# Weight sums of a seven-product matrix pair: from VectorE additions to accumulating DMA transfers

## The chip, the cores and the metric

The kernel runs on one core of a Trainium2 chip. The metric is the device time of one execution in microseconds, from the program's first to its last instruction on the core, with what the launch adds around it. Engines are named as in the profile: PE is TensorE's matrix multiply, DVE is VectorE, ACT is ScalarE, POOL is GpSimd, and SP is the engine whose queue issues most DMA transfers.

## The reference

One inference step of a two-layer decoder trunk for 536 tokens (16 learned tokens, 512 of a prompt, 8 of a sample group). Each layer has a half feed-forward block, a recurrent mixer and a second half feed-forward block, so there are four feed-forward blocks of this form:

```python
def half_ffn(x, g, w_gate, w_up, w_down):
    h = rmsnorm(x, g)
    return 0.5 * ((jax.nn.silu(h @ w_gate) * (h @ w_up)) @ w_down)
```

The model width is 1024 and the hidden width 2816, all in float32. The change touches only how `h @ w_gate` and `h @ w_up` are formed.

## The kernel before

Every float32 product is made of three matrix multiplies with rounded operands. A weight tile is split into a rounded high part (`whi`, a cast on ACT) and a remainder (`wlo`, a subtraction on DVE), and likewise the activations (`hh`, `hl`). `block_mm` then issues high times high, high times low and low times high (lines 328 to 330).

A feed-forward block walks over 22 column tiles of 128 hidden units, in pieces of 8, 8 and 6; after each piece come four items that multiply with `w_down`. The first four column tiles of a block are done plainly (`run_plain`), the other 18 with a scheme of seven half products in place of eight (`seven_item` and `run_seven`). So each block has groups of 4, 8 and 6 such tiles in a row, and the program has 72. Such a tile is called an item below. Its gate weights g and up weights u are loaded as two tiles of 512 KB (`raw`, or `rawx` for every second item), each with two halves g0, g1 and u0, u1 of 128 by 512 numbers. The scheme needs the weights w (g0 and g1), u1, and the sums

- t1 = g0 + u0,
- t2 = t1 + u1,
- t4 = t2 + g1,
- s = u0 + u1.

All four sums are made on DVE, by `sums_a` (lines 342 and 343) and `sums_b` (lines 348 and 349), into one tile `wsum`; `split` turns each into a high and a low part.

The seven products of an item stand on PE in a fixed order, called P1 to P7 here, each of 12 matrix multiplies. They run over PSUM banks a, b and c. Bank a takes P1, P3, P5 and P7, and between them it is read out: by `keep` (line 484, a copy on ACT) after P1 and after P3, by line 507 on DVE after P5, and by line 513 on ACT after P7. P2 goes to bank b, which line 496 reads on DVE. P4 and P6 go to bank c. While one item is multiplied, the steps of the next one (its sums and splits) are called one after another between the products by `nstep`, and `load_next` issues the load of the item after that into the raw tiles that have come free.

The kernel gives the program order; the tile framework's scheduler then lays down a fixed order for each engine, which can differ from the order of the calls. An engine takes its instructions strictly in that order: one that waits holds up everything queued behind it.

Of the kernel before, what the change touches and what calls it, by code (L numbers as in the profile page):

```python
# [11 lines left out]
F32 = mybir.dt.float32  # L12
# [3 lines left out]
ALU = mybir.AluOpType  # L16
# [89 lines left out]
def trunk(ctx, tc, A, O):  # L106
    nc = tc.nc
    P = 128
    cnt = [0]

    def til(pool, shape, tag, dt=F32, bufs=None):
        cnt[0] += 1
        kw = {} if bufs is None else {"bufs": bufs}
        return pool.tile(shape, dt, tag=tag, name=f"{tag}_{cnt[0]}", **kw)
# [17 lines left out]
    def bank(tag="m"):  # L132
        return til(rings[tag][0], [P, 512], tag)
# [135 lines left out]
    ext = {}  # L269
    turn = {"raw": 0, "whi": 0, "wlo": 0}  # L270

    def wtile(tag):
        n = turn[tag]
        turn[tag] = n + 1
        dt = F32 if tag == "raw" else F32R
        if ext and n % 4 > 1:
            return til(ext["pool"], [P, 2, 512], f"{tag}x", dt, bufs=2)
        return til(wpool, [P, NK, P], tag, dt, bufs=2).rearrange("p (h k) m -> p h (k m)", h=2)
# [4 lines left out]
    def split_w(src):  # L283
        n = src.shape[1]
        hi, lo = wtile("whi")[:, :n], wtile("wlo")[:, :n]
        nc.scalar.copy(hi, src)
        nc.vector.tensor_sub(lo, src, hi.bitcast(F32))  # L287
        return hi, lo

    def load_pair(it, srcs, nk):  # L290
        it.raw = [wtile("raw") for _ in srcs]
        for t, src in zip(it.raw, srcs):
            dst = t.rearrange("p h (k m) -> p (h k) m", m=P)[:, :nk]
            nc.sync.dma_start(dst, src.rearrange("(k p) m -> p k m", p=P))
# [25 lines left out]
    def pair_item(wg, wu, j):  # L320
        return plain_item([w[:, 128 * j:128 * j + 128] for w in (wg, wu)], NK)


    def block_mm(o, u, nk, rh, rl, start, stop):
        hi, lo = u
        kw = {} if start else {"skip_group_check": True}
        for k in range(nk):
            nc.tensor.matmul(o, hi[:, k], rh(k), start=start and k == 0, stop=False, **kw)  # L328
            nc.tensor.matmul(o, hi[:, k], rl(k), start=False, stop=False, **kw)  # L329
            nc.tensor.matmul(o, lo[:, k], rh(k), start=False, stop=stop and k == nk - 1, **kw)  # L330
# [3 lines left out]
    def seven_item(wg, wu, j):  # L334
        it = Item()
        it.w = {}
        it.load = lambda: load_pair(it, [w[:, 128 * j:128 * j + 128] for w in (wg, wu)], NK)

        def sums_a():
            g, u = it.raw  # L340
            it.t = t = til(ext["pool"], [P, 4, 512], "wsum", bufs=1)
            nc.vector.tensor_add(t[:, 1], g[:, 0], u[:, 0])
            nc.vector.tensor_add(t[:, 0], t[:, 1], u[:, 1])

        def sums_b():
            g, u = it.raw
            t = it.t
            nc.vector.tensor_add(t[:, 2], u[:, 0], u[:, 1])
            nc.vector.tensor_add(t[:, 3], t[:, 0], g[:, 1])

        def split(name, src):
            def fn():
                it.w[name] = split_w(src())
            return fn

        it.steps = [sums_a, split("w", lambda: it.raw[0]), split("t", lambda: it.t[:, 0:2]), sums_b]
        it.late = [split("s", lambda: it.t[:, 2:4]), split("u", lambda: it.raw[1][:, 1:2])]
        return it

    def ffn(l, pre, rstd, first=None, done=None, start=None, tokens=PARTS, scaled_end=None):  # L360
# [5 lines left out]
        n = a1 - a0  # L366
        t1, t2, tl = slice(a0, a1), slice(b0, b1), slice(a0, b1)
# [6 lines left out]
        def flush():  # L374
            while pending:
                pending.pop(0)()
# [3 lines left out]
        with tc.tile_pool(name="ffn", bufs=2) as fp:  # L380
# [5 lines left out]
            def hidden(gt, ut):  # L386
                h = gtile(F32R)
                hid.append(h)

                def fn():  # L390
                    nc.vector.tensor_mul(ut[:, tl], ut[:, tl], gt[:, tl])
                    nc.scalar.copy(h[:, 0, tl], ut[:, tl])
                    nc.vector.tensor_sub(h[:, 1, tl], ut[:, tl], h[:, 0, tl].bitcast(F32))

                pending.append(fn)
# [69 lines left out]
            def run_seven(it, j, nxt):  # L465
                gt, ut = til(fp, [P, T], "gt"), til(fp, [P, T], "ut")
                bank_of = {}

                def product(b, name, i, rh, rl, first, last):
                    if first:  # L470
                        bank_of[b] = bank("d")[:, :n]
                    u = tuple(z[:, i].rearrange("p (k m) -> p k m", m=P) for z in it.w[name])
                    block_mm(bank_of[b], u, 4, rh, rl, first, last)
                    return bank_of[b]

                def half_x(h, ts):
                    return (lambda k: hh[:, 4 * h + k, ts]), (lambda k: hl[:, 4 * h + k, ts])

                def half_s(i):
                    return (lambda k: Z["h"][:, i, k]), (lambda k: Z["l"][:, i, k])  # L480

                def keep(ps):
                    s = til(fp, [P, n], "part", bufs=4)
                    nc.scalar.copy(s, ps)  # L484
                    return s

                def nstep():
                    if nxt is not None and nxt.steps:
                        nxt.steps.pop(0)()

                pa = product("a", "w", 0, *half_x(0, t1), True, True)
                s1 = keep(pa)
                it.late[0]()
                flush()
                pb = product("b", "w", 1, *half_x(1, t1), True, True)
                nc.vector.tensor_add(gt[:, t1], pb, s1)
                nc.scalar.activation(gt[:, t1], gt[:, t1], AF.Silu)
                it.late[1]()
                pa = product("a", "t", 0, *half_s(1), False, True)
                s2 = keep(pa)  # L500
                load_next()
                nstep()
                pc = product("c", "t", 1, *half_s(0), True, True)
                s3 = keep(pc)
                nstep()
                pa = product("a", "s", 0, *half_s(2), False, True)
                nc.vector.tensor_add(ut[:, t2], pa, s3)
                nstep()
                pc = product("c", "u", 0, *half_s(3), False, True)
                nc.vector.tensor_add(ut[:, t1], pc, s2)  # L510
                nstep()
                pa = product("a", "s", 1, *half_x(1, t2), False, True)
                nc.scalar.activation(gt[:, t2], pa, AF.Silu)
                hidden(gt, ut)

# [21 lines left out]
            for k0, k1 in PIECES:  # L537
                for j in range(k0, k1):
                    if j < PLAIN:
                        it = first if j == 0 and first is not None else pair_item(wg, wu, j)  # L540
                        items.append((it, lambda it, nxt, j=j: run_plain(it, j, nxt)))
                    else:
                        items.append((seven_item(wg, wu, j), lambda it, nxt, j=j: run_seven(it, j, nxt)))
                if k1 == FT:
                    def close(it, nxt):
                        sp.close()
                        if scaled_end is not None:
                            scaled_end()

                    items.append((None, close))  # L550
                for parts in ([tokens[:1], tokens[1:]] if ends and k1 == FT else [tokens]):
                    for m in range(0, NK, 2):
                        srcs = [wd[128 * k0:128 * k1, 128 * (m + i):128 * (m + i) + 128] for i in range(2)]
                        items.append((plain_item(srcs, k1 - k0),
                                      lambda it, nxt, k0=k0, k1=k1, m=m, parts=parts: run_down(it, k0, k1, m, parts, nxt)))
# [5 lines left out]
            def load_next():  # L561
                if loads:
                    loads.pop(0).load()
# [1107 lines left out]
```

## Time and profile before

| | |
|---|---|
| median of 3 runs | 2327.33 us (2322.22 to 2327.39) |
| the profiled execution | 2327.36 us |
| its span, first to last instruction | 2325.6 us |
| PE busy | 2275.5 us, 98% of the span |
| DVE busy | 1669.8 us, 72% |
| ACT busy | 1080.4 us, 46% |
| POOL busy | 142.0 us, 6% |

The profiled execution stands at the median of the runs; 1.8 us of it lie around the span. Busy shares are averages over stages with different limits: the feed-forward blocks, the mixers and the ends have to be read apart.

### The profile page before, as it was taken

To read this page: it belongs to the slowest core of one execution; us is meant where nothing else is said; L and a number is where in the kernel's file an instruction comes from. 1 tells how busy PE (TensorE), PEld (TensorE's weight loads), DVE (VectorE), ACT (ScalarE), POOL (GpSimd) and SP (SyncE) were. 2 spreads that over 40 slices of the span, in tenths; PEclk is the share of its full clock that TensorE was granted. 3 is DMA by queue.
4 is the path that set the end of the run, shared out by engine and by line. 5 is a ranking of instruction groups with operands and counts; after the bars stand their busy time and mean duration, and the time that the engine had idled before them with its cause. 6 is when DMAs were issued, how large, how long until landed. Compare 5 with 4: busy or idle time off the path is not lost. (4 is left out here: it accounts for less than half of the span.)

```text
span 2325.6 us, 45180 instructions
## 1 busy us (share of the span) xinstructions
PE 2275.5 (98%) x18368; PEld 2226.7 (96%) x18368; DVE 1669.8 (72%) x2980; ACT 1080.4 (46%) x2040; POOL 142.0 (6%) x192
## 2 busy tenths in 40 slices
PE   8999999999999999999999999999999999999998
PEld 8999999989998988999999999999999989999998
DVE  7858476696656787966757885847666877958576
ACT  6525254373343456434535452525433455525355
POOL 0000000312212100000000000000021200000000
PEclk9999999999999999999999999999999999999999
DMA  6323334222222116242423332333344454233324
GB/s 177 109 74 103 90 96 135 82 66 79 79 71 70 49 41 174 70 121 75 118 75 99 91 110 81 101 92 95 116 120 116 124 166 141 85 98 100 109 85 135
DMA packets 417849, 233.71 MB, mean 100 GB/s; under 512 B 19397, under 2 KB 408838, under 8 KB 417641
## 3 DMA queue, kind: packets, MB, share of 16 engines
q1 hardware_dynamic: 416920, 229.40, 34.1%
q8 instruction: 144, 2.36, 0.4%
q10 hardware_dynamic: 720, 1.42, 0.2%
q14 instruction: 65, 0.52, 0.1%
HBM read 215.81 MB, written 14.97 MB: 99 GB/s over the span
## 5 line engine op out<-in xcount | busy, mean ns | idle before, releaser
L234 PE MATMUL d<-hh,whi 128*128 128x264 f32 (+2 forms) x1136 | 343.7, 303 | 5.8 <-ACT whi L222 3.8
L236 PE MATMUL d<-hh,wlo 128*128 128x264 f32 (+2 forms) x1136 | 327.0, 288 | 1.8 <-DVE wlo L223 1.7
L235 PE MATMUL d<-hl,whi 128*128 128x264 f32 (+2 forms) x1136 | 326.3, 287 | 1.4 <-DVE hl L1404 1.4
L329 PE MATMUL d<-hl,whi 128*128 128x268 f32 (+1 forms) x832 | 238.4, 287 | 1.8 <-DVE hl L187 1.7
L328 PE MATMUL d<-hh,whi 128*128 128x268 f32 (+1 forms) x832 | 237.3, 286 | 1.7 <-ACT hh L186 1.2
L330 PE MATMUL d<-hh,wlo 128*128 128x268 f32 (+1 forms) x832 | 237.6, 286 | 0.5 <-DVE wlo L287 0.5
L234 PEld LDWEIGHTS d<-hh,whi 128*128 128x128 f32 x1136 | 216.2, 190 | 11.5 <-ACT whi L222 5.1
L236 PEld LDWEIGHTS d<-hh,wlo 128*128 128x128 f32 x1136 | 215.3, 190 | 4.8 <-DVE wlo L223 4.1
L235 PEld LDWEIGHTS d<-hl,whi 128*128 128x128 f32 x1136 | 216.2, 190 | 1.8 <-DVE hl L1404 1.6
L528 DVE SCALAR_TENSOR_TENSOR xT<-d,xT 128x272 f32<-128x272 f32 (+2 forms) x192 | 83.0, 434 | 167.0 <-PE d L330 166.9
L328 PE MATMUL d<-hid,whi 128*128 128x264 f32 (+2 forms) x704 | 201.5, 287 | 0.0
L328 PE MATMUL d<-hid,whix 128*128 128x264 f32 (+2 forms) x704 | 201.1, 286 | 0.0
L329 PE MATMUL d<-hid,whix 128*128 128x264 f32 (+2 forms) x704 | 200.8, 285 | 0.0
L329 PE MATMUL d<-hid,whi 128*128 128x264 f32 (+2 forms) x704 | 200.7, 286 | 0.0
L330 PE MATMUL d<-hid,wlox 128*128 128x264 f32 (+2 forms) x704 | 200.6, 285 | 0.0
L330 PE MATMUL d<-hid,wlo 128*128 128x264 f32 (+2 forms) x704 | 200.4, 285 | 0.0
L222 ACT CAST whi<-raw 128x512 fp32r<-128x512 f32 (+1 forms) x158 | 99.0, 662 | 160.6 <-PE d L235 103.2
L328 PE MATMUL d<-sumh,whix 128*128 128x268 f32 (+1 forms) x576 | 170.3, 296 | 0.2 <-ACT part L484 0.2
L328 PE MATMUL d<-sumh,whi 128*128 128x268 f32 (+1 forms) x576 | 164.4, 285 | 0.0
L330 PE MATMUL d<-sumh,wlo 128*128 128x268 f32 (+1 forms) x576 | 164.2, 285 | 0.0
L329 PE MATMUL d<-suml,whi 128*128 128x268 f32 (+1 forms) x576 | 164.2, 285 | 0.0
L329 PE MATMUL d<-suml,whix 128*128 128x268 f32 (+1 forms) x576 | 163.9, 285 | 0.0
(381 smaller groups left out, 6699.0 us busy)
## 6 DMA issues: line engine op xcount, KB each, us to landing
raw<-in_ffn_gate_dram SPq DMA_DIRECT2D x44, 512.0 KB
raw<-in_ffn_up_dram SPq DMA_DIRECT2D x44, 512.0 KB
rawx<-in_ffn_gate_dram SPq DMA_DIRECT2D x44, 512.0 KB
rawx<-in_ffn_up_dram SPq DMA_DIRECT2D x44, 512.0 KB
raw<-in_ffn_down_dram SPq DMA_DIRECT2D x32, 512.0 KB
rawx<-in_ffn_down_dram SPq DMA_DIRECT2D x32, 512.0 KB
raw<-in_even_w_in_dram SPq DMA_DIRECT2D x30, 512.0 KB
raw<-in_odd_w_in_dram SPq DMA_DIRECT2D x25, 512.0 KB
```

Source lines behind the costliest of these rows:

```text
L222: nc.scalar.copy(hi[:, ks], raw[:, ks])
L234: nc.tensor.matmul(o, hi[:, k], h, start=(k == 0), stop=False)
L235: nc.tensor.matmul(o, hi[:, k], l, start=False, stop=False)
L236: nc.tensor.matmul(o, lo[:, k], h, start=False, stop=(k == nk - 1))
L328: nc.tensor.matmul(o, hi[:, k], rh(k), start=start and k == 0, stop=False, **kw)
L329: nc.tensor.matmul(o, hi[:, k], rl(k), start=False, stop=False, **kw)
L330: nc.tensor.matmul(o, lo[:, k], rh(k), start=False, stop=stop and k == nk - 1, **kw)
L528: nc.vector.scalar_tensor_tensor(xv[:, sl], ps, -0.5, xv[:, sl], ALU.mult, ALU.add)
```

## The change

One sum, t1, is still made on DVE (line 343 of the changed kernel). The other three are made in place by DMA transfers that POOL issues and that add what they carry to what lies at their destination:

- s: half u1 is added onto half u0 within the raw tile of u (line 344),
- t2: once t1 has been split, half u1 is added onto the tile that holds t1 (line 359),
- t4: once t2 has been split, half g1 is added onto the same tile (line 359 again).

The sum tile shrinks from four halves to one, and there are two of them in turn. The splits become: t1, w, t2 during the item before, and u (both halves, now s and u1) and t4 during the item's own products. The third and fourth product now use t2 and t1 under their own names, in the same order as before.

```diff
-        def sums_a():
-            g, u = it.raw
-            it.t = t = til(ext["pool"], [P, 4, 512], "wsum", bufs=1)
-            nc.vector.tensor_add(t[:, 1], g[:, 0], u[:, 0])
-            nc.vector.tensor_add(t[:, 0], t[:, 1], u[:, 1])
-
-        def sums_b():
-            g, u = it.raw
-            t = it.t
-            nc.vector.tensor_add(t[:, 2], u[:, 0], u[:, 1])
-            nc.vector.tensor_add(t[:, 3], t[:, 0], g[:, 1])
-
-        def split(name, src):
+
+        def first_sum():
+            g, u = it.raw
+            it.t = til(ext["pool"], [P, 512], "wsum")
+            nc.vector.tensor_add(it.t, g[:, 0], u[:, 0])
+            nc.gpsimd.dma_start(u[:, 0], u[:, 1], accum_op=ALU.add)
+
+        def split(name, i):
             def fn():
-                it.w[name] = split_w(src())
+                if i is not None:
+                    it.w[name] = split_w(it.raw[i])
+                    return
+                n = 0 if name != "t2" else 1
+                if n == 0:
+                    it.slot = wtile("whi"), wtile("wlo")
+                hi, lo = (z[:, n] for z in it.slot)
+                it.w[name] = tuple(z[:, n:n + 1] for z in it.slot)
+                nc.scalar.copy(hi, it.t)
+                nc.vector.tensor_sub(lo, it.t, hi.bitcast(F32))
+                if name != "t4":
+                    nc.gpsimd.dma_start(it.t, (it.raw[1] if name == "t1" else it.raw[0])[:, 1], accum_op=ALU.add)
             return fn
 
-        it.steps = [sums_a, split("w", lambda: it.raw[0]), split("t", lambda: it.t[:, 0:2]), sums_b]
-        it.late = [split("s", lambda: it.t[:, 2:4]), split("u", lambda: it.raw[1][:, 1:2])]
+        it.steps = [first_sum, split("t1", None), split("w", 0), split("t2", None)]
+        it.late = [split("u", 1), split("t4", None)]
...
-                it.late[1]()
-                pa = product("a", "t", 0, *half_s(1), False, True)
+                nstep()
+                pa = product("a", "t2", 0, *half_s(1), False, True)
                 s2 = keep(pa)
                 load_next()
-                nstep()
-                pc = product("c", "t", 1, *half_s(0), True, True)
+                it.late[1]()
+                pc = product("c", "t1", 0, *half_s(0), True, True)
...
-                pa = product("a", "s", 0, *half_s(2), False, True)
+                pa = product("a", "u", 0, *half_s(2), False, True)
...
-                pc = product("c", "u", 0, *half_s(3), False, True)
+                pc = product("c", "u", 1, *half_s(3), False, True)
...
-                pa = product("a", "s", 1, *half_x(1, t2), False, True)
+                pa = product("a", "t4", 0, *half_x(1, t2), False, True)
```

**DVE in the middle of a group of eight.** The first block, second group: the item being multiplied has the tiles `gt_338` and `ut_339` and the banks `d_340`, `d_344` and `d_351`. Before the change, over the length of one item, from the first sum of the next item (`wsum_350`) on:

```order
L342 TENSOR_TENSOR wsum_350_2534<-raw_328_2401,raw_329_2402 128x512
L348 TENSOR_TENSOR wsum_350_2534<-raw_329_2402 128x512
L393 TENSOR_TENSOR hid_337_2472<-ut_319_2345,hid_337_2472 128x536
L496 TENSOR_TENSOR gt_338_2473<-d_344_2497,part_341_2488 128x268
L343 TENSOR_TENSOR wsum_350_2534<-wsum_350_2534,raw_329_2402 128x512
L287 TENSOR_TENSOR wlo_354_2553<-raw_328_2401,whi_353_2552 128x1024
L349 TENSOR_TENSOR wsum_350_2534<-wsum_350_2534,raw_328_2401 128x512
L287 TENSOR_TENSOR wlo_356_2570<-wsum_350_2534,whi_355_2569 128x1024
L507 TENSOR_TENSOR ut_339_2474<-d_340_2475,part_352_2570 128x268
L510 TENSOR_TENSOR ut_339_2474<-d_351_2537,part_347_2528 128x268
```

After the change, at the same item. `wsum_325` is its own sum tile, `wsum_345` that of the next item and `wsum_365` that of the item after next; line 357 subtracts in a split of t1, t2 or t4, line 287 in one of w or u:

```order
L357 TENSOR_TENSOR wlox_350_2554<-wsum_325_2401,whix_349_2553 128x512
L502 TENSOR_TENSOR gt_338_2493<-d_344_2517,part_341_2508 128x268
L357 TENSOR_TENSOR wlo_354_2573<-wsum_345_2532,whi_353_2572 128x512
L343 TENSOR_TENSOR wsum_365_2663<-rawx_347_2549,rawx_348_2550 128x512
L287 TENSOR_TENSOR wlo_356_2591<-raw_327_2418,whi_355_2590 128x1024
L513 TENSOR_TENSOR ut_339_2494<-d_340_2495,part_352_2570 128x268
L357 TENSOR_TENSOR wlo_354_2573<-wsum_345_2532,whi_353_2572 128x512
L516 TENSOR_TENSOR ut_339_2494<-d_351_2557,part_346_2547 128x268
L287 TENSOR_TENSOR wlox_363_2642<-raw_328_2419,whix_362_2641 128x1024
L397 TENSOR_TENSOR ut_339_2494<-ut_339_2494,gt_338_2493 128x536
L399 TENSOR_TENSOR hid_357_2623<-ut_339_2494,hid_357_2623 128x536
L357 TENSOR_TENSOR wlox_370_2685<-wsum_345_2532,whix_369_2684 128x512
```

Three additions per item have gone. The first sum has moved ahead: before, it was that of the next item and stood ahead of the read-out of bank b; now it is that of the item after next and stands between the next item's t1 split and its w split, ahead of the read-out of bank a (line 513, line 507 before). The splits of t1, t2 and t4 of one tile stand 4 and 5 rows apart.

**ACT at the same place after the change,** from the item's own t4 cast (`whix_349`) to the read-out of bank a after P7 (line 519). Line 356 casts t1, t2 or t4, line 286 w or u, and line 490 is the copy in `keep`:

```order
L356 CAST whix_349_2553<-wsum_325_2401 128x512
L356 CAST whi_353_2572<-wsum_345_2532 128x512
L503 ACTIVATE gt_338_2493<-gt_338_2493 128x268
L490 COPY part_346_2547<-d_340_2495 128x268
L286 CAST whi_355_2590<-raw_327_2418 128x1024
L490 COPY part_352_2570<-d_351_2557 128x268
L356 CAST whi_353_2572<-wsum_345_2532 128x512
L286 CAST whix_362_2641<-raw_328_2419 128x1024
L519 ACTIVATE gt_338_2493<-d_340_2495 128x268
```

The next item's t1 cast now stands right behind this item's t4 cast, and its t2 cast ahead of its u cast; before, there was one cast for two sums in each of two places.

**POOL over the same stretch after the change** (before, it had nothing in the feed-forward blocks): every row is one accumulating transfer of 256 KB.

```order
L359 DMA wsum_325_2401<-rawx_308_2288 128x512
L344 DMA raw_328_2419<-raw_328_2419 128x512
L359 DMA wsum_325_2401<-rawx_307_2287 128x512
L359 DMA wsum_345_2532<-raw_328_2419 128x512
L344 DMA rawx_348_2550<-rawx_348_2550 128x512
L359 DMA wsum_345_2532<-raw_327_2418 128x512
```

Three transfers per item have come, in the order t2 of the next item, s of the item after next, t4 of the next item.

## Rows read from the trace of the kernel before

**Rows 1.** The page, part 1: busy us (share of the span) xinstructions.

```profile
PE 2275.5 (98%) x18368; PEld 2226.7 (96%) x18368; DVE 1669.8 (72%) x2980; ACT 1080.4 (46%) x2040; POOL 142.0 (6%) x192
```

**Rows 2.** Busy time by stretch: length, busy (instructions) of each engine, PEclk, DMA.

```profile
200.00:400.00 200.00, 200.00 (x1610) 198.67 (x1610) 135.68 (x203) 90.00 (x140) 1.78 (x4) 1.00 0.35 105
400.00:600.00 200.00, 193.46 (x1547) 182.96 (x1546) 147.97 (x294) 98.94 (x207) 48.56 (x72) 1.00 0.27 77
...
1200.00:1400.00 200.00, 200.00 (x1605) 198.90 (x1605) 156.93 (x237) 103.29 (x161) 0.00 (x0) 1.00 0.35 100
```

**Rows 3.** Instructions on the sum tile: duration ns min/median/max, first and last start.

```profile
L342 DVE TENSOR_TENSOR wsum<-raw,raw x36: 682/687/700, 57.2 to 2249.3; 128x512 f32<-128x512 f32 x36
...
L342 DVE TENSOR_TENSOR wsum<-rawx,rawx x36: 683/686/693, 73.8 to 2259.5; 128x512 f32<-128x512 f32 x36
```

**Rows 4.** Timeline of PE: P1, P3, P7 of one item, the next P1.

```profile
1117.41 0.29 PE L328 MATMUL d<-hh,whi 128*128 128x268 f32 x1
...
1120.37 0.29 PE L328 MATMUL d<-sumh,whi 128*128 128x268 f32 x1
...
1126.43 0.29 PE L328 MATMUL d<-hh,whix 128*128 128x268 f32 x1
...
1127.91 0.28 PE L328 MATMUL d<-hh,whi 128*128 128x268 f32 x1
```

**Rows 5.** Timeline of ACT in the same item: start us, us, what, [idle before].

```profile
1117.49 0.62 ACT L286 CAST whix<-rawx 128x512 fp32r<-128x512 f32 x1 [0.37 <-PE d L329]
...
1120.49 1.05 ACT L286 CAST whi<-raw 128x1024 fp32r<-128x1024 f32 x1 [0.21 <-PE d L329]
...
1126.56 1.05 ACT L286 CAST whix<-wsum 128x1024 fp32r<-128x1024 f32 x1 [1.77 <-issue]
```

**Rows 6.** Timeline of DVE in the same item.

```profile
1118.29 0.69 DVE L287 TENSOR_TENSOR wlox<-rawx,whix 128x512 fp32r<-128x512 f32 x1
...
1119.52 0.69 DVE L342 TENSOR_TENSOR wsum<-raw,raw 128x512 f32<-128x512 f32 x1
...
1121.35 0.43 DVE L496 TENSOR_TENSOR gt<-d,part 128x268 f32<-128x268 f32 x1
1121.70 0.68 DVE L343 TENSOR_TENSOR wsum<-wsum,raw 128x512 f32<-128x512 f32 x1
1122.30 1.22 DVE L287 TENSOR_TENSOR wlo<-raw,whi 128x1024 fp32r<-128x1024 f32 x1
1123.43 0.69 DVE L349 TENSOR_TENSOR wsum<-wsum,raw 128x512 f32<-128x512 f32 x1
...
1127.64 1.23 DVE L287 TENSOR_TENSOR wlox<-wsum,whix 128x1024 fp32r<-128x1024 f32 x1 [0.57 <-ACT whix L286]
```

**Rows 7.** Timeline of SP's queue: four transfers at their issue.

```profile
355.40 0.34 SPq L1465 DMA_DIRECT2D xd<-xT  x1
...
592.52 0.40 SPq L1073 DMA_DIRECT2D acc<-in_state_rwkv_dram  x1
...
654.28 0.39 SPq L1073 DMA_DIRECT2D acc<-in_state_rwkv_dram  x1
...
1031.83 0.37 SPq L294 DMA_DIRECT2D raw<-in_ffn_up_dram  x1
```

**Rows 8.** Timelines of POOL and DVE: the instructions that waited for the last three.

```profile
595.60 1.28 POOL L1077 TENSOR_TENSOR sq<-acc,sq 128x512 f32<-128x512 f32 x1 [33.88 <-DMA acc<-in_state_rwkv_dram]
...
657.48 1.27 POOL L1077 TENSOR_TENSOR sq<-acc,sq 128x512 f32<-128x512 f32 x1 [19.30 <-DMA acc<-in_state_rwkv_dram]
...
1035.91 0.69 DVE L342 TENSOR_TENSOR wsum<-raw,raw 128x512 f32<-128x512 f32 x1 [2.87 <-DMA raw<-in_ffn_up_dram]
```

**Rows 9.** DMA by quarter us after the first: length, PEclk, DMA share, GB/s.

```profile
356.25:356.50 0.25, 1.00 0.93 360
356.50:356.75 0.25, 1.00 1.01 394
356.75:357.00 0.25, 1.00 0.83 326
```

## The prediction

> **What bounds the kernel now.** I read the page's busy times first: PE is busy for 2275.5 of 2325.6 us, DVE for 1669.8 [rows 1]. Then I read busy times by stretch, because an average hides which stage has gaps. In the feed-forward stretches PE is busy for 200.00 of 200 us, with DVE at 136 to 157; only mixer stretches leave PE idle, 6.5 us in the one shown [rows 2]. All 72 changed items lie where PE has no gap. One item takes 10.50 us from its P1 to the next one's P1 on PE [rows 4]. DVE work taken away there shortens nothing; the question is whether the new transfers make PE wait.
>
> **What the change removes.** Three of four additions on DVE, 0.69 us each [rows 3], issued 0.60 us apart (1121.70 to 1122.30 in [rows 6]): 1.8 us per item, 130 us over 72. PE covers all of it, so I put it at nothing. It would be worth something only where PE waits for DVE. ACT's and DVE's columns for the splits are the same as before, and PE's work is unchanged.
>
> **What it adds: two transfers in a chain.** Before, t1 and t2 were ready together. Now the t2 transfer can start only when t1's split has read the tile, and t4's only when t2's split has. L is the time from a transfer's issue on POOL to the moment an instruction that waits for it starts. I count from P1 of the item being multiplied, and the sums are those of the next one:
>
> - The t1 cast goes into the slot of this item's w, so it starts when P2 ends: 2.96 (1120.37 less 1117.41, [rows 4]), and 0.12 later, as the w cast did at 1120.49 [rows 5]: 3.08. It takes 0.62; from a cast's end to its subtraction 0.03 pass (1126.56 and 1.05 are 1127.61; DVE starts at 1127.64 in [rows 6]); the subtraction takes 0.69. T1 is split at 4.42, and the t2 transfer is issued.
> - T2 lands at 4.42 + L; cast, handover and subtraction are 0.62 + 0.03 + 0.69 = 1.34, and the t4 transfer is issued at 5.76 + L.
> - T4 lands at 5.76 + 2L. In both queues its split stands ahead of the t1 split of the item after: cast 0.62 and 0.03 on ACT and to DVE, then on DVE t4's subtraction 0.60, the bank b read-out 0.35 and t1's subtraction 0.69. That t1 is split at 8.05 + 2L.
>
> From one t1 split to the next is thus 2L + 3.63 us. PE's item is 10.50. If the loop is longer, each item slips by 2L - 6.87.
>
> **How long L is.** No transfer from POOL and no accumulating one stands in this trace. The nearest rows are plain transfers from SP's queue [rows 7, 8]: 256 KB with 2 KB per partition took 3.08 us from issue to its waiting instruction (592.52 to 595.60), and 3.20 another time; 512 KB took 4.08 (1031.83 to 1035.91). An accumulating transfer has to read its destination too, so it moves like more than 256 KB: I take 4.05, which is 3.15 plus the 0.9 that another 256 KB adds in those rows. The low end is 3.08, nothing added. For the high end I take two passes one after the other, 6.2. To one of the two L comes a share: t2 is issued at 4.4, when the 1 MB of weights for the item after next is also on its way. 268 KB keep the DMA engines busy for 0.75 us at 326 to 394 GB/s [rows 9], so I add half of that, 0.4. The slip per item is then 2L - 6.47: 1.63 us at L = 4.05.
>
> **What the slip costs.** Behind the t1 subtraction DVE's queue holds the first sum of the item after next (0.60), the w split (1.13, 1122.30 to 1123.43 in [rows 6]) and the read-out of bank a (0.43), for which P7 waits. With no slip the subtraction starts at 3.73, the read-out ends at 3.73 + 0.60 + 0.60 + 1.13 + 0.43 = 6.49, and P7 starts at 9.02 (1126.43 less 1117.41, [rows 4]): 2.53 us of slack. The first item of a group gets its sums during the `w_down` products ahead, so a group of n items has n - 2 loops. At 1.63 per loop: 6 x 1.63 - 2.53 = 7.25 us for a group of eight, 4 x 1.63 - 2.53 = 3.99 for six, 2 x 1.63 - 2.53 = 0.73 for four; 11.97 per block, **47.9 us** for four blocks. A second path gives nearly the same: the load of the item after next but one half waits for t4's landing (it takes over g's tile), and its own 4.08 plus 0.60, 1.13 and 0.43 end at 5.76 + 2L - 10.50 + 6.24, which is 9.6 at L = 4.05 against P7 at 9.02; from there it slips alike. I don't add it. Nothing is won back between groups, since PE has no gaps there.
>
> Sum: 2327.4 (the profiled execution, which is the median to 0.1 us) + 48 = **2375 us**. At L = 3.6 the same lines give 9 us, at 4.6 they give 101: the likeliest case alone runs from 2336 to 2428.
>
> **Rivals.** *Hidden:* with the share counted, loops stall only if six slips exceed 2.53, that is above L = 3.45. If the transfer adds little to the 3.08 to 3.20 of a plain one, the time stays at 2327, within 4. For it: the plain rows lie below that point, and both ends here are on-chip. Against it: a second read of 256 KB and descriptors that POOL has to make.
>
> The Trainium skill gives, in "DMA: Bandwidth & Descriptors", section "Anatomy of one DMA — SWDGE (gpsimd) path", about 2.0 us plus the bytes at 436 GB/s for a transfer issued by GpSimd; as an estimate that is 2.6 us for 256 KB, and by it nothing would be late. The same sum for 512 KB is 3.2 where this trace shows 4.08 on SP's queue, so I trust it little here. The page also says, under "Rules for kernel authors", that an accumulating transfer reads its destination and writes it later, for which it gives no time.
>
> *Much later:* L above 4.9, by slow descriptor making or two passes. At L = 5.3 the slip is 4.13 per loop: 22.25 + 13.99 + 5.73 = 41.97 per block, 168 in all, 2495 us; at L = 6.2 it is 254, 2582 us.
>
> *The load is late, whatever L is:* the first sum now needs the load a whole item earlier than before. U's split waits for P6's end (its slot): cast to 9.02 + 0.12 + 1.05 = 10.19, subtraction to 11.45, which is 0.95 in the next item. Then 1 MB is loaded: 4.08, and about 1.5 for the second half at some 350 GB/s, so the first sum starts at 6.5 and the bank read-out ends at 8.7, 0.3 ahead of P7. If t2's transfer takes 0.75 of that, 0.42 is over, and half of it is paid per item (the ring comes round every second item). First sums placed so are 5, 3 and 1 in groups of eight, six and four, 36 in four blocks: 36 x 0.21 = 8 us, 2335. The margin is thin; without the sharing it is zero.
>
> *Faster:* PE waits for DVE where a block hands over to the next stage, and DVE, 1.8 us per item lighter, gets there earlier. It decides only if the transfers are hidden and such a wait ends last; the six items of a block's last group are worth 11 us of DVE, four times. Against it: PE is gapless through the blocks, and in handovers DVE follows PE's last products. If it closed the 6.5 us of gaps of the mixer stretch shown [rows 2] at two handovers, that would be 13 us, 2314. That the sums aren't taken off DVE can't be: its rows show them gone.
>
> **Numbers.** Chances: late transfers as summed 0.46, hidden 0.22, much later 0.20, late load alone 0.08, faster 0.04. A time within 0.3% (7 us) of before can't be told from it. Slower by more: 0.46 + 0.20 + 0.08 = 0.74; same 0.22; faster 0.04. The range starts below the hidden case, at 2324, and goes to L of 5.6 (slip 4.73: 49 per block, 197), rounded up to 2530; about half of the much-later case and the faster one stay outside.
>
> **What will show it.** In the profile after: DVE busy some 130 us less; PE with gaps within the items of a group, at P7 first, that end with line 513 of DVE; ACT and DVE waiting on DMA at lines 356 and 357; the interval between P1s near 12.1 us from the third item of a group of eight on, and 10.5 at its start. Time from a POOL transfer's issue to the cast that waits for it gives L. I am wrong if these casts find their data there (L below 3.4), if P7's wait ends with the first sum's load and not with the loop, or if items of a group stall from the first one on, which would mean that something else than the chain sets the pace.

## The result, and the profile after

The changed kernel took 2398.49 us (median of 4 runs, 2397.32 to 2401.96); the kernel before took 2325.3 us beside it. The ratio is 1.032, with a 95% interval of 1.030 to 1.033: slower by 73 us, where 48 were forecast, and inside the range. Page of the profile after, busy times and the new transfers (last column: median us from issue to landing):

```profile
PE 2295.6 (96%) x18368; PEld 2234.0 (93%) x18368; DVE 1550.8 (65%) x2836; ACT 1080.9 (45%) x2112; POOL 328.6 (14%) x408
...
wsum<-raw POOLq DMA_DIRECT2D x72, 256.0 KB, 3.7
wsum<-rawx POOLq DMA_DIRECT2D x72, 256.0 KB, 3.6
```

Beside [rows 1], DVE is 119 us lighter, and the span has grown from 2325.6 to 2396.0 us all the same. The stretches that were gapless in [rows 2] (same columns) show where:

```profile
200.00:400.00 200.00, 194.45 (x1548) 191.86 (x1547) 115.99 (x174) 88.24 (x148) 24.96 (x29) 1.00 0.59 140
...
1200.00:1400.00 200.00, 195.61 (x1563) 193.75 (x1562) 132.26 (x208) 92.33 (x150) 22.38 (x26) 1.00 0.50 118
```

PE has lost 5.55 and 4.39 us per 200 us, at the same granted clock (1.00 in all four rows). What PE and DVE waited for (total us, times, longest):

```profile
PE d L328 <- DVE ut L513: 26.9, 35, 1.6
PE d L328 <- ACT part L490: 19.2, 29, 2.0
...
DVE wsum L343 <- DMA rawx<-in_ffn_up_dram: 75.8, 32, 3.2
...
DVE wsum L343 <- DMA raw<-in_ffn_up_dram: 52.0, 24, 2.9
```

The first sum's waits in the kernel before (line 342 there):

```profile
DVE wsum L342 <- DMA raw<-in_ffn_up_dram: 23.0, 8, 3.4
```

PE now waits for the read-out of bank a (line 513, before P7) and for the copy of `keep` (line 490). The first sum waited for its load 56 times out of 72; before, it did so 8 times. Of these 56 loads, 39 were issued as the t4 transfer landed and 16 as u's split ended. Each of PE's 35 waits behind line 513 follows a first sum that waited for its load. One item of the second group of eight, in the same block as [rows 4 to 6], all engines:

```profile
1127.22 0.29 PE L328 MATMUL d<-sumh,whi 128*128 128x268 f32 x1
...
1129.52 0.68 DVE L357 TENSOR_TENSOR wlo<-wsum,whi 128x512 fp32r<-128x512 f32 x1
...
1130.49 0.86 POOL L359 DMA_DIRECT2D wsum<-raw  x1 [5.56 <-DVE wlo L357]
...
1131.82 0.69 DVE L343 TENSOR_TENSOR wsum<-rawx,rawx 128x512 f32<-128x512 f32 x1 [1.61 <-DMA rawx<-in_ffn_up_dram]
...
1133.56 0.43 DVE L513 TENSOR_TENSOR ut<-d,part 128x268 f32<-128x268 f32 x1
...
1134.05 0.39 PE L328 MATMUL d<-hh,whix 128*128 128x268 f32 x1 [0.44 <-DVE ut L513]
...
1134.19 0.62 ACT L356 CAST whi<-wsum 128x512 fp32r<-128x512 f32 x1 [2.56 <-DMA wsum<-raw]
...
1135.83 0.86 POOL L359 DMA_DIRECT2D wsum<-raw  x1 [2.17 <-DVE wlo L357]
...
1138.65 0.40 PE L328 MATMUL d<-sumh,whi 128*128 128x268 f32 x1
...
1139.55 0.37 SPq L294 DMA_DIRECT2D raw<-in_ffn_up_dram  x1
1139.61 0.62 ACT L356 CAST whix<-wsum 128x512 fp32r<-128x512 f32 x1 [1.01 <-DMA wsum<-raw]
...
1142.19 0.86 POOL L359 DMA_DIRECT2D wsum<-rawx  x1 [5.50 <-DVE wlo L357]
```

Both paths of the prediction can be read here. **The chain:** t1's subtraction ends at 1130.20, the t2 transfer is issued at 1130.49, its cast starts 3.70 us later, the t4 transfer is issued at 1135.83 with its cast 3.78 later, and the next t2 transfer goes out at 1142.19. The loop is 11.70 us, against 10.50 for PE's item before. **The load:** the up load is issued at 1139.55, in the moment in which t4 has landed (its cast starts at 1139.61). The load that fed this item's first sum waited likewise, so the sum at 1131.82 started after a wait of 1.61 us, line 513 behind it ended at 1133.99, and P7 started after a wait of 0.44. From P3 to P3 this item took 11.43 us.

### The profile page after: what moved, and what is told of

The parts are those of the page before. It is cut to its first block, busy times and chain, and to the rows that moved or that the text cites. A ratio compares the mean times of both kernels' runs of the same rounds, so it can differ in the third digit from the quotient of the medians.

```text
span 2396.0 us, 45862 instructions
## 1 busy us (share of the span) xinstructions
PE 2295.6 (96%) x18368; PEld 2234.0 (93%) x18368; DVE 1550.8 (65%) x2836; ACT 1080.9 (45%) x2112; POOL 328.6 (14%) x408
## 5 line engine op out<-in xcount | busy, mean ns | idle before, releaser
L328 PE MATMUL d<-hh,whi 128*128 128x268 f32 (+1 forms) x880 | 252.6, 288 | 3.7 <-ACT hh L186 3.2
L330 PE MATMUL d<-hh,wlo 128*128 128x268 f32 (+1 forms) x880 | 252.7, 288 | 0.4 <-DVE wlo L287 0.4
L328 PE MATMUL d<-hid,whix 128*128 128x264 f32 (+2 forms) x874 | 250.1, 287 | 1.9 <-ACT hid L398 1.8
L329 PE MATMUL d<-hid,whix 128*128 128x264 f32 (+2 forms) x874 | 249.2, 286 | 0.0
L330 PE MATMUL d<-hid,wlox 128*128 128x264 f32 (+2 forms) x874 | 248.7, 285 | 0.0
L234 PEld LDWEIGHTS d<-hh,whi 128*128 128x128 f32 x1136 | 216.1, 190 | 12.2 <-ACT whi L222 5.8
L236 PEld LDWEIGHTS d<-hh,wlo 128*128 128x128 f32 x1136 | 215.2, 190 | 4.3 <-DVE wlo L223 3.7
L235 PEld LDWEIGHTS d<-hl,whi 128*128 128x128 f32 x1136 | 216.3, 190 | 1.8 <-DVE hl L1410 1.6
L356 ACT CAST whi<-wsum 128x512 fp32r<-128x512 f32 x156 | 96.6, 619 | 220.3 <-DMA wsum<-raw 104.2
L328 PE MATMUL d<-sumh,whix 128*128 128x268 f32 (+1 forms) x576 | 171.9, 299 | 16.2 <-ACT part L490 15.8
L328 PEld LDWEIGHTS d<-hh,whi 128*128 128x128 f32 x880 | 167.2, 190 | 4.4 <-ACT hh L186 3.6
L328 PE MATMUL d<-hh,whix 128*128 128x268 f32 (+1 forms) x496 | 145.3, 293 | 26.9 <-DVE ut L513 26.9
L329 PEld LDWEIGHTS d<-hl,whi 128*128 128x128 f32 x880 | 167.0, 190 | 2.2 <-DVE hl L187 2.0
L328 PEld LDWEIGHTS d<-hid,whix 128*128 128x128 f32 x874 | 164.3, 188 | 4.2 <-ACT hid L398 4.1
L330 PEld LDWEIGHTS d<-hh,wlo 128*128 128x128 f32 x880 | 167.2, 190 | 0.8 <-DVE wlo L287 0.7
```

What stands on the lines that cost most here:

```text
L234: nc.tensor.matmul(o, hi[:, k], h, start=(k == 0), stop=False)
L235: nc.tensor.matmul(o, hi[:, k], l, start=False, stop=False)
L236: nc.tensor.matmul(o, lo[:, k], h, start=False, stop=(k == nk - 1))
L356: nc.scalar.copy(hi, it.t)
```

## The experiments

Theory A is the chain of two landings, theory B the load that waits for t4's landing and holds the first sum. All times are medians beside runs of the kernel before on the same chip (2326.8 to 2327.1).

**e1: all three sums on DVE, in the new places.**

```diff
-            nc.gpsimd.dma_start(u[:, 0], u[:, 1], accum_op=ALU.add)
+            nc.vector.tensor_add(u[:, 0], u[:, 0], u[:, 1])
...
-                    nc.gpsimd.dma_start(it.t, (it.raw[1] if name == "t1" else it.raw[0])[:, 1], accum_op=ALU.add)
+                    nc.vector.tensor_add(it.t, it.t, (it.raw[1] if name == "t1" else it.raw[0])[:, 1])
```

> All three in-place sums are made by DVE additions at the places where the transfers stood; buffers, order of the splits and order of the products are those of the changed kernel. The chain's two landings become two additions of 0.69 us, so its loop is 2 x 0.69 + 3.63 = 5.0 us against PE's 10.50. If the transfers make the time (by the chain of two landings, or by the load that waits for the second of them), this runs within 10 us of before: 2320 to 2335. If the new order and the smaller sum tile make it, it stays near 2398.

Measured: 2363.19 us, ratio 1.016 [1.014, 1.018]; between the two expectations. Half the loss is there with no transfer at all. Timelines:

```profile
1134.91 0.69 DVE L343 TENSOR_TENSOR wsum<-rawx,rawx 128x512 f32<-128x512 f32 x1 [1.79 <-DMA rawx<-in_ffn_up_dram]
1135.52 0.68 DVE L359 TENSOR_TENSOR wsum<-wsum,raw 128x512 f32<-128x512 f32 x1
...
1136.24 0.62 ACT L356 CAST whi<-wsum 128x512 fp32r<-128x512 f32 x1 [2.62 <-DVE wsum L359]
...
1137.71 0.37 ACT L490 COPY part<-d 128x268 f32<-128x268 f32 x1
...
1138.14 0.40 PE L328 MATMUL d<-sumh,whix 128*128 128x268 f32 x1 [1.99 <-ACT part L490]
```

The load was issued at 1129.55, as u's split ended: the first sum is late though no transfer from POOL delays it. Behind it in DVE's order stands t2's addition, t2's cast on ACT waits for that addition, and `keep`, for which PE waits, stands behind the cast. `keep` is PE's largest wait here (22.5 us in 23 pieces; line 513 has 3.8 in 5). The order is not that of the changed kernel, against what was expected: there the w cast and `keep` stand ahead of t2's cast. So e1 shows a late load and a new order together.

**e2: only t4 on DVE.**

```diff
-                if name != "t4":
-                    nc.gpsimd.dma_start(it.t, (it.raw[1] if name == "t1" else it.raw[0])[:, 1], accum_op=ALU.add)
+                if name == "t1":
+                    nc.gpsimd.dma_start(it.t, it.raw[1][:, 1], accum_op=ALU.add)
+                if name == "t2":
+                    nc.vector.tensor_add(it.t, it.t, it.raw[0][:, 1])
```

> Only the t4 sum is made by a DVE addition, s and t2 stay with transfers. One landing is left in the loop: 3.74 + 0.29 + 0.69 + 3.63 = 8.35 us, below PE's 10.50. Chain of two landings: the stalls go nearly whole, 2325 to 2340. Load that waits for t4's landing: also gone, since g's half is read by DVE at once, 2325 to 2340. If instead every transfer costs about its share (DMA engines or POOL shared), a third of the 73 us goes: about 2374.

Measured: 2339.41 us, ratio 1.0055 [1.0037, 1.0073]. 59 of the 73 us go with one of the three transfers, so they don't share the cost equally. But its loop was not 8.35 us, as two issues of t2's transfer on POOL and the cast between them show:

```profile
1117.48 0.86 POOL L359 DMA_DIRECT2D wsum<-rawx  x1 [7.93 <-DVE wlo L357]
...
1120.76 0.62 ACT L356 CAST whi<-wsum 128x512 fp32r<-128x512 f32 x1 [1.49 <-DMA wsum<-rawx]
...
1128.08 0.86 POOL L359 DMA_DIRECT2D wsum<-raw  x1 [7.78 <-DVE wlo L357]
```

They are 10.60 us apart, 3.28 to the cast and 7.32 from there on. In these 7.32 us DVE and ACT wait for one another and never for PE. In DVE's fixed order u's split and the hidden step (gate times up, lines 399 and 401) stand between t4's addition and the next t1 split, so a loop that on paper has 2 us to spare just keeps step with PE. The load stays late as well, now behind u's split (52 of 54 late loads), and the 11 waits of PE behind line 513 (515 here) all follow such a first sum:

```profile
PE d L328 <- DVE ut L515: 7.2, 11, 2.1
```

**e3: a third pair of weight tiles.**

```diff
+        if ext and tag == "raw" and n % 6 > 1:
+            return til(ext["pool"], [P, 2, 512], "rawx", dt, bufs=4)
-        if ext and n % 4 > 1:
+        if ext and tag != "raw" and n % 4 > 1:
...
-                    s = til(fp, [P, n], "part", bufs=4)
+                    s = til(fp, [P, n], "part", bufs=3)
```

> A third pair of weight tiles, so the load of the item after next need not wait until the t4 transfer has read g (to make room, the partial sums that ACT copies out have three buffers in place of four). The chain of the two landings is untouched. Chain theory: its loop of 11.70 us stays longer than PE's 10.50, so the time stays within 15 us of the changed kernel, 2383 to 2400. Load theory: P7's wait, which in the trace ends behind a first sum that waited for its load, goes away, and the time falls to about 2335.

Measured: 2380.57 us, ratio 1.0232 [1.0216, 1.0247]: 18 us less than the changed kernel, three more than the edge A gave. The largest wait of PE:

```profile
PE d L330 <- ACT part L492: 28.8, 71, 1.9
```

The chain on POOL's and ACT's timelines:

```profile
1132.66 0.86 POOL L361 DMA_DIRECT2D wsum<-rawx  x1 [5.57 <-DVE wlo L359]
...
1136.05 0.62 ACT L358 CAST whi<-wsum 128x512 fp32r<-128x512 f32 x1 [2.31 <-DMA wsum<-rawx]
...
1141.94 0.62 ACT L358 CAST whix<-wsum 128x512 fp32r<-128x512 f32 x1 [1.48 <-DMA wsum<-rawx]
...
1144.52 0.86 POOL L361 DMA_DIRECT2D wsum<-raw  x1 [5.97 <-DVE wlo L359]
```

The first sum waits for its load 16 times, each time a load issued as u's split ended. PE does not wait for line 513 (515 here) any more, and the loop still takes 11.86 us. What is late next is `keep` (now line 492), which stands behind the casts that wait for t4 and t2 in ACT's queue. (Three buffers for the partial sums are not the reason: e10 has three as well and waits 4.1 us for `keep`.) The chain alone holds most of the loss; the load has a share of its own.

**e4: one sum tile in place of two.**

```diff
-            it.t = til(ext["pool"], [P, 512], "wsum")
+            it.t = til(ext["pool"], [P, 512], "wsum", bufs=1)
```

> One sum tile in place of two. The first sum of an item must now follow the t4 split of the item before it, so it is made a whole item later and finds its load landed; the loop gets longer by the first sum's 0.69 us and a handover, to some 12.7 us. Chain theory: slower than the changed kernel, 2425 to 2450 (slip 2.2 in place of 1.2 us per loop). Load theory: the wait for the load is gone, so faster than the changed kernel, about 2345.

Measured: 2472.47 us, ratio 1.063 [1.061, 1.064]. The direction is A's, and B as sole cause falls: the first sum waited for its load only 8 times, as before the change. The size is past A's figure. The loop is 13.14 us where 12.7 was worked out (the two t2 transfers below, on POOL's timeline), and PE's largest wait is 94.0 us in 86 pieces, for `keep`:

```profile
1152.03 0.86 POOL L359 DMA_DIRECT2D wsum<-raw  x1 [0.57 <-DVE wlo L357]
...
1165.17 0.86 POOL L359 DMA_DIRECT2D wsum<-rawx  x1 [0.57 <-DVE wlo L357]
```

```profile
PE d L328 <- ACT part L490: 94.0, 86, 4.4
```

**e5: e1 with e3's third pair** (both diffs above).

> The first run (all sums made by DVE, no transfer) with the third pair of weight tiles. The first run took 36 us more than before although nothing waits for POOL; its trace shows the early first sum waiting for its load. If that load is the whole of it, the third pair takes it away: 2323 to 2335. If the new order of the splits or the in-place additions hold PE up, it stays at 2355 to 2365.

Measured: 2337.74 us, ratio 1.0045 [1.0030, 1.0060]. This is above the range for a load that is all of it. The third pair takes 25 of e1's 36 us away, though not by the load alone: the scheduler's order of DVE and ACT is not that of e1 either. Some 11 us stay with no transfers and with late loads only at the 16 places that e3 has too.

**e6: e2 with e3's third pair.**

> The second run (s and t2 by transfers, t4 by DVE) with the third pair of weight tiles. One landing per loop (8.35 us) and no load that waits for a split: chain theory and load theory together leave nothing to wait for, 2323 to 2333. If each transfer has a cost of its own on POOL or the DMA engines, some of the 12 us of the second run stays: 2335 to 2340.

Measured: 2355.31 us, ratio 1.0122 [1.0107, 1.0137]: a miss, 16 us above e2 where less was expected. The third pair also changed the scheduler's order (the first sum moved ahead of t1's subtraction, between the two rows of the hidden step), t2's transfers were issued 10.92 us apart in the stretch below, and PE waited 28 times, 12.1 us, for `keep`:

```profile
1248.55 0.86 POOL L361 DMA_DIRECT2D wsum<-rawx  x1 [0.90 <-DVE wlo L359]
...
1252.15 0.62 ACT L358 CAST whi<-wsum 128x512 fp32r<-128x512 f32 x1 [1.68 <-DMA wsum<-rawx]
...
1259.47 0.86 POOL L361 DMA_DIRECT2D wsum<-rawx  x1 [10.07 <-DVE wlo L359]
```

So a loop that was level with PE in e2 has become longer than PE's item. From the cast on it takes 7.32 us, as in e2; what is longer in these stretches is the way from issue to cast, 3.60 us in place of 3.28. Why that is longer, and what the new order costs elsewhere, stays open.

**e7: plain copies in place of the additions.**

```diff
-            nc.gpsimd.dma_start(u[:, 0], u[:, 1], accum_op=ALU.add)
+            nc.gpsimd.dma_start(u[:, 0], u[:, 1])
...
-                    nc.gpsimd.dma_start(it.t, (it.raw[1] if name == "t1" else it.raw[0])[:, 1], accum_op=ALU.add)
+                    nc.gpsimd.dma_start(it.t, (it.raw[1] if name == "t1" else it.raw[0])[:, 1])
```

> The same three transfers from POOL at the same places, but plain copies in place of accumulating ones, so the three additions are left out of the computation; all else is that of the changed kernel. If accumulating is what makes a landing long (as the estimate had it: 3.15 plain, 0.9 for reading the destination), issue to landing falls from a median of 3.7 to about 3.1 us, the loop to 2 x 3.1 + 0.58 + 3.63 = 10.4 us, under PE's 10.50, and the time to that of the late load alone, 2350 to 2368. If accumulating costs nothing beside a copy, the time stays within 5 us of 2398 and the landing at 3.6 to 3.7.

Measured: 2352.34 us, ratio 1.0103 [1.0086, 1.0120]. The page's row of half of the copies (the other half reads the same):

```profile
wsum<-raw POOLq DMA_DIRECT2D x72, 256.0 KB, 2.3
```

A copy of 256 KB lands in 2.3 us (median) where the accumulating transfer took 3.6 to 3.7, and DVE and ACT keep the changed kernel's order but for one row. That takes 46 us off; 25 stay, with the first sum waiting for its load 56 times as in the changed kernel, and PE's largest wait is for line 513 (9.6 us in 16 pieces, each behind such a first sum).

**e8: only s on DVE** (the first pair of lines of e1's diff).

> Only the sum s goes back to DVE; t2 and t4 stay transfers. s is no link of the chain, so by the chain theory the loop stays at 11.7 us and the time at 2390 to 2405. If the three transfers hinder each other on POOL or the DMA engines (s is issued right after the t2 transfer), landings get shorter and a part of the 73 us goes: 2375 to 2385.

Measured: 2405.23 us, ratio 1.034 [1.032, 1.036]: as A had it, s is no link of the chain. The 7 us over the changed kernel are little beside the spread of these runs, but they fit B: on DVE the addition of s stands between the late first sum and line 513, which is 2.48 us behind it in place of 1.74 (1131.82 to 1133.56), and PE's 35 waits for line 513 come to 44.2 us in place of 26.9:

```profile
1127.85 0.69 DVE L343 TENSOR_TENSOR wsum<-rawx,rawx 128x512 f32<-128x512 f32 x1 [1.56 <-DMA rawx<-in_ffn_up_dram]
...
1130.33 0.43 DVE L513 TENSOR_TENSOR ut<-d,part 128x268 f32<-128x268 f32 x1
```

**e9: t2 and t4 carry half the columns.**

```diff
-                    nc.gpsimd.dma_start(it.t, (it.raw[1] if name == "t1" else it.raw[0])[:, 1], accum_op=ALU.add)
+                    nc.gpsimd.dma_start(it.t[:, :256], (it.raw[1] if name == "t1" else it.raw[0])[:, 1, :256], accum_op=ALU.add)
```

> The t2 and t4 transfers carry only the first 256 of 512 columns (128 KB in place of 256), so half of these two additions is left out; s stays whole. If the landing grows with the bytes (the estimate took the second 256 KB of reading at 0.9 us), a landing falls from 3.7 to about 2.9 us, the loop to 2 x 2.9 + 0.58 + 3.63 = 10.0, below 10.50, and the time to about that of the plain copies, 2345 to 2365. If accumulating costs a fixed time whatever the size, landings stay above 3.4 us and the time at 2380 to 2400.

Measured: 2369.96 us, ratio 1.0193 [1.0173, 1.0213]. On the sum tile:

```profile
DMA to landing us min/median/max: 2.6/2.7/4.7
```

The landing grows with the bytes, as expected; in the changed kernel the same view gives 3.2/3.7/5.7. The time is 5 us above the range given: the loop by formula is under 10.50, but PE still waited 18 times for `keep` and 5 times for line 513. The scheduler's order changed here too, so it is not a test of the bytes alone.

**e10: e7 with e3's third pair.**

> Plain copies (the three additions left out) and the third pair of weight tiles together. In the run with plain copies issue to use was about 2.3 to 2.8 us where nothing else shared, so the loop of two landings is 2 x 2.5 + 0.58 + 3.63 = 9.2 us, under 10.50, and no load waits for a split. Chain and load theory together: 2328 to 2342, about that of the run with all sums on DVE and the third pair (2338). If the third pair does harm by itself, as the run of e6 against e2 (2355 against 2339) may mean, it is above 2352.

Measured: 2338.62 us, ratio 1.0049 [1.0035, 1.0064]; as expected. Its order on DVE and ACT is that of e3, row by row. With short landings and no load that waits for t4, about as much is left (12 us) as in e5 (11); that the cause is the same is not shown.

**e11: less work for DVE in the kernel before.**

```diff
-            nc.vector.tensor_add(t[:, 2], u[:, 0], u[:, 1])
-            nc.vector.tensor_add(t[:, 3], t[:, 0], g[:, 1])
...
-        it.late = [split("s", lambda: it.t[:, 2:4]), split("u", lambda: it.raw[1][:, 1:2])]
+        it.late = [split("s", lambda: it.t[:, 0:2]), split("u", lambda: it.raw[1][:, 1:2])]
```

> The kernel before with two of its four additions left out (s and t4; the split of t1 and t2 is made twice in their place), so DVE has 1.2 us less to do per item, some 90 us in all. The first step of the prediction put such relief at nothing, since PE has no gaps there: within 5 us of before, 2322 to 2332. If DVE's queue holds PE up in places that the stretches shown don't hold, it is faster by more: 2300 to 2318.

Measured: 2328.40 us, ratio 1.0006 [0.9997, 1.0015]. DVE does 81 us less than in [rows 1], and nothing comes of it:

```profile
PE 2280.5 (98%) x18368; PEld 2230.9 (96%) x18368; DVE 1588.4 (68%) x2836; ACT 1083.3 (47%) x2040; POOL 143.2 (6%) x192
```

**e12: only t2 on DVE.**

```diff
-                if name != "t4":
-                    nc.gpsimd.dma_start(it.t, (it.raw[1] if name == "t1" else it.raw[0])[:, 1], accum_op=ALU.add)
+                if name == "t1":
+                    nc.vector.tensor_add(it.t, it.t, it.raw[1][:, 1])
+                if name == "t2":
+                    nc.gpsimd.dma_start(it.t, it.raw[0][:, 1], accum_op=ALU.add)
```

> The mirror of the second run: t2 is made by DVE, s and t4 by transfers. Again one landing per loop. By the chain theory alone the time is that of the second run, 2335 to 2345. But here the load of the item after next still waits for a landing, that of t4, where in the second run g's half was read by DVE at once. If the load theory has its share, this run is slower than the second by 10 us or more: 2350 to 2370.

Measured: 2424.17 us, ratio 1.041 [1.040, 1.043]: slower than e2 by 85 us, far past what either theory gave, and slower than the changed kernel with a transfer less. Timelines:

```profile
1155.50 0.37 SPq L294 DMA_DIRECT2D rawx<-in_ffn_up_dram  x1
...
1161.32 0.69 DVE L343 TENSOR_TENSOR wsum<-rawx,rawx 128x512 f32<-128x512 f32 x1 [1.36 <-DMA rawx<-in_ffn_up_dram]
1161.93 0.69 DVE L359 TENSOR_TENSOR wsum<-wsum,raw 128x512 f32<-128x512 f32 x1
...
1162.65 0.62 ACT L356 CAST whi<-wsum 128x512 fp32r<-128x512 f32 x1 [2.09 <-DVE wsum L359]
...
1164.12 0.37 ACT L492 COPY part<-d 128x268 f32<-128x268 f32 x1
...
1164.54 0.39 PE L328 MATMUL d<-sumh,whix 128*128 128x268 f32 x1 [1.46 <-ACT part L492]
```

In DVE's order t2's addition of the next item stands behind the first sum of the item after next, which waits for its load; t2's cast, and behind it the w cast and `keep` in ACT's queue, wait for that addition; PE waits for `keep`. So the late load reaches a second engine, as in e1, and which instruction stands behind the late one sets its price. It is no test of B as worded, though: most late loads here were issued as u's split ended (37 of 53, that at 1155.50 among them), only 4 as t4 landed, and t2's cast has moved ahead of the w cast and `keep`, which the changed kernel has the other way round.

## Why the prediction was right, and where it was not

The difference can be laid out by four runs, each a step from the one before it: kernel before 2326.8; e10 2338.6 (new order, third pair, short landings); e3 2380.6 (landings as accumulating transfers); changed kernel 2398.5 (two pairs). That is 12 us for the order with the third pair, 42 for the chain, 18 for the load. These steps hold little else: without buffer numbers, e3 and e10 have the same order of instructions on DVE and ACT, e3 and the changed kernel differ in some 40 of DVE's 2836 rows and 12 of ACT's 2112. (In e1, e2, e4, e5, e6, e9 and e12 the scheduler moved over a hundred rows, so their differences hold order as well.) The shares depend on the path: with plain copies (e7 less e10) the load is worth 14, with the sums on DVE (e1 less e5, other order included) 25.

By groups, from PE's timeline: us by which the intervals from one P3 to the next (n - 1 in a group of n) are longer than before, four blocks together. In the changed kernel they hold 62.7 of the 70.4 us by which the span grew:

| | groups of 4 | of 8 | of 6 |
|---|---|---|---|
| forecast | 2.9 | 29.0 | 16.0 |
| changed kernel | 19.5 | 27.4 | 15.8 |
| e3, chain without the late load | 12.4 | 20.3 | 11.1 |
| e10, neither | 4.4 | 1.9 | -0.2 |

- **The removed DVE work is worth nothing:** right, and shown by e11. DVE's relief was 119 us and not 130, since a split of two sums in one (1.23 us, [rows 6]) became two of 0.69: 0.15 us per item, 11 us in all, which the line "the columns are the same" left out.
- **L = 4.05:** right in the sum, in part by luck. From issue to cast it was 3.70 and 3.78; with the 0.29 us from the end of a subtraction to POOL's issue, which was not counted, 4.03 in the mean. In its parts: accumulating costs 1.3 us over a copy (3.6 to 2.3; 0.9 was taken), and a copy from POOL lands after 2.3 where 3.15 was taken from SP's loads. The added 0.4 for sharing was not in the item read; instead landings reach 5.7 us in some items.
- **The loop and its slip:** right as a bound. 2L + 3.63 with the measured L is 11.69, and 11.70 was read (the forecast had 12.13, with L = 4.05 and the share of 0.4). The step assumed that a loop below 10.50 costs nothing. e2, e6 and e9 are below it on paper and still lose time: in e2 and e6 the in-order queues put rows into the loop that the sum of the links does not hold (10.60 and 10.92 read, 8.35 worked out); e9 is open.
- **P7 first, behind line 513:** the place is right for 35 waits, the path to it is not. All 35 follow a first sum that waited for its load, which is the second path, and which the prediction named as a sign of being wrong ("if P7's wait ends with the first sum's load and not with the loop"). With the load out of the way but the loop as long (e3), PE never waits for that line. The loop costs time at `keep`: 29 waits in the changed kernel, 71 in e3, none foreseen. ACT's queue holds casts that wait for landings ahead of a copy that PE needs.
- **Groups of eight and six:** 43.2 us against 45.0, partly by luck: the forecast put all of it on the chain, but the chain alone (e3 less e10) makes 29.6 of it, and the load, put at nothing, 11.8 (changed kernel less e3). Nor did the slack at a group's start come as forecast: in the group of eight read above the intervals are 11.31, 11.66, 11.35, 11.43, 11.63, 12.77 and 10.49 us, longer than before from the first one on (the other three such groups start at 10.2 to 10.5).
- **Groups of four:** this is the term that failed by most, 2.9 forecast and 19.5 measured. "The first item of a group gets its sums during the `w_down` products ahead" isn't so there: a block's first group follows plain column tiles. The timelines after show its first item's chain running while the item itself is being multiplied (its P3 starts at 71.41):

```profile
71.49 0.86 POOL L359 DMA_DIRECT2D wsum<-raw  x1 [4.11 <-DVE wlo L357]
...
76.07 0.37 SPq L294 DMA_DIRECT2D raw<-in_ffn_up_dram  x1
76.08 0.62 ACT L356 CAST whix<-wsum 128x512 fp32r<-128x512 f32 x1 [2.32 <-DMA wsum<-raw]
...
77.55 0.37 ACT L490 COPY part<-d 128x268 f32<-128x268 f32 x1
...
77.97 0.39 PE L328 MATMUL d<-sumh,whix 128*128 128x268 f32 x1 [1.96 <-ACT part L490]
```

  Its t4 lands only at 76.08, the load for the item after next starts in the same moment, and `keep`, in ACT's queue behind the t4 cast, holds P5 up by 1.96 us. So a group of four pays chain and load from its first item on, with no slack of 2.53 us to use up first; stalls from the first item on were the prediction's other sign of being wrong.
- **The second path, "I don't add it":** a term put at nothing that was worth 18 us (changed kernel less e3). Chain and load touch different waits (line 513 with the load, `keep` without it), so removing one leaves the other. The rival that priced the late load at 8 us started it at u's split; in the changed kernel that holds for 16 of the 56 late loads, in e1 and e2 for nearly all. Its margin of 0.3 us was too good: it took one duration, while loads that the first sum waited for took from 3.8 to 6.2 us in the trace after.
- **The hidden rival** would have failed even with its short transfers. The Trainium skill, "DMA: Bandwidth & Descriptors", section "Anatomy of one DMA — SWDGE (gpsimd) path", gives by its fit some 2.6 us for 256 KB as an estimate. A plain copy from POOL agrees roughly (2.3 us, e7); the accumulating transfer at 3.6 to 3.7 is above it; and e7, whose transfers are as short as the fit, is still 25 us slower than before.

What stays open: the 11 to 12 us of e5 and e10, some 6 of which lie within the groups in e10 (table), the excess of e6 over e2, and what e9 still loses. No version tried is faster than the kernel before, and with PE gapless in these stretches none had time there to win.

## What to carry to other kernels

Taking work off an engine that the gapless engine never waits for buys nothing, and what it is exchanged for can only cost. An in-place update by a transfer turns independent sums into a chain: add up handover, landing and every queue entry from one link to the next, compare that with the time of one item, and count what the fixed order of each queue puts between the links (in e2 that made 10.60 us of 8.35). A step that is moved one item ahead brings its load one item ahead too; ask what stands behind it in each in-order queue, and work out groups by what really precedes them.

## What the runs showed of the hardware

- An accumulating on-chip transfer of 256 KB from POOL landed after 3.2/3.7/5.7 us (minimum, median, maximum), a copy of the same size after 2.2/2.3/4.8, an accumulating one of 128 KB after 2.6/2.7/4.7. By the minima, accumulating costs 1.0 us at 256 KB, and half the bytes save 0.6.
- Most accumulating transfers kept POOL busy for 0.86 us each (1.0 in a few), and in the item read POOL issued 0.29 us after the subtraction that released it. The copies of e7 bring POOL's busy time from 328.6 to 260.5 us, 0.32 us less for each of 216 transfers.
